# A hybrid decoder layer on one core: recurrent gates' products moved, and the mixer's VectorE and ScalarE work put in a fixed order

## The chip, the cores and the metric

The kernel runs on one core of a Trainium2 chip. The metric is the device time of one execution in microseconds (us), taken as the median of the runs.

## The reference

The layer is a SwiGLU half-step, a token mixer, and a second SwiGLU half-step, each behind an RMS norm, for 512 tokens of width 1024. The change concerns the mixer alone.

```
def hybrid_mixer(h, w_in, ..., w_out):
    z = h @ w_in
    c_val, c_gate, r_x, r_gate = jnp.split(z, [W_CONV, 2 * W_CONV, 2 * W_CONV + W_LRU], axis=-1)
    u = c_val * jax.nn.sigmoid(c_gate)
    u = causal_depthwise_conv(u, conv_dw, conv_dw_bias)            # 31 taps
    u = jax.nn.silu(layernorm(u, conv_ln_g, conv_ln_b))
    xr = causal_depthwise_conv(r_x, lru_conv_w, lru_conv_b)        # 4 taps
    yr = rg_lru(xr, lru_w_a, lru_b_a, lru_w_x, lru_b_x, lru_lambda)
    yr = yr * jax.nn.gelu(r_gate, approximate=True)
    return jnp.concatenate([u, yr], axis=-1) @ w_out

def rg_lru(x, w_a, b_a, w_x, b_x, lam):
    r = jax.nn.sigmoid(block_diag_linear(x, w_a, b_a))
    i = jax.nn.sigmoid(block_diag_linear(x, w_x, b_x))
    log_a = -LRU_C * r * jax.nn.softplus(-lam)
    a = jnp.exp(log_a)
    mult = jnp.sqrt(-jnp.expm1(2.0 * log_a))
    h_t = a_t * h_(t-1) + mult_t * (i_t * x_t)     # a scan over the tokens
```

## The kernel before

Everything is in float32 of which each matrix operand is split into a high half (rounded to the fast matmul type) and a low half (the rest). A product then takes three passes: high by high, high by low, low by high. ScalarE makes the high halves (casts), VectorE the low ones (subtractions). Channels lie on the partitions, in tiles of 128; the mixer has four tiles (c = 0 to 3) of the convolution group and four of the recurrent group, with 512 tokens each. PSUM has eight banks, used in turn by all stages.

The mixer runs in this order on TensorE. First the convolution's gate and value products of the tiles 0, 1 and 2, then the recurrent inputs (`rx_units`), then gate and value of the fourth tile (`zc_units(3)`), all into banks called pz; then the four recurrent gate products (`rg_units`, also pz), called rg0 to rg3 here. In between lie the recurrent gates' small block-diagonal products (pga), which `lru` issues. Last comes the output projection (`out_units`, banks po), first its recurrent half (yhi, ylo by the weight slabs hl), then the convolution's half (uhi, ulo). Between its parts stand the sums over channels with a matrix of ones (pm): the mean, then the variance, of the convolution's output.

The 31 taps of the convolution run on VectorE for the tiles 0, 2 and 3 (`conv_dve`, two PSUM accumulators pc, result cv) and on ScalarE and GpSimd for tile 1 (`conv_pool`). When a VectorE tile has its value product (the product of value bank and gate sigmoid, `val_out`), its taps are queued in `convs`; `step_convs` issues them as long as a planned VectorE clock is behind TensorE's. `lru` is a chain, a generator that is advanced once for each 2.72 us of planned TensorE work: eight gate products (pga) with a sigmoid each (r, i); GpSimd's product xr by i; on ScalarE tanh (th), exponential (r) and square (i); on VectorE the sum th = (i + 1) th; the square root on ScalarE; GpSimd's product xr by th; VectorE's scans (th from r and xr, two tiles a pair); the gating th by gl, where gl is the gelu of the recurrent gate products; the cast yhi and the low half ylo. The constant SCAN_LATER holds the scans back by five such steps. `layernorm` subtracts the mean (cv - pm), squares (sq), takes the variance's root (rs), the reciprocal by token halves, multiplies, applies Silu with gain and bias, casts to uhi and subtracts to ulo.

The calls of `tc.keep_in_program_order` (pin) hold an instruction at the place among the pinned ones of its engine where it is written. All others are placed by a scheduler, by the priority under which they were issued. SP's queue carries the loads of the weight slabs; the slabs of the output projection (wso) and of the second half-step (raw) take their buffers as older slabs come free.

Of the kernel before, what the change touches and what calls it, by code (L numbers as in the profile page):

```python
# [13 lines left out]
P = 128  # L14
# [24 lines left out]
PR_SIDE = -400  # L39
PR_OUT = 300  # L40
PR_COMB = 0
SCAN_LATER = 5
RMS_EPS = 1e-6
LN_EPS = 1e-5
A, B, ALL = (0, HT), (HT, HT), (0, T)
# [30 lines left out]
def layer_kernel(ctx: ExitStack, tc, x, gains, w_g1, w_u1, w_d1a, w_d1b, w_in,  # L76
# [66 lines left out]
    def step_chains():  # L143
        for c in list(chains):
            with tc.high_priority(offset=c[0]):
                if next(c[1], None) is None:
                    chains.remove(c)

    def step_convs():
        while convs and clock["dve"] < clock["pe"]:  # L150
            with tc.high_priority(offset=PR_CONV):
                us = next(convs[0], None)
            if us is None:
                convs.pop(0)
            else:
                dve(us)
# [479 lines left out]
    def zc_units(c, parts):  # L636
        off = ASIDE if len(parts) == 2 else 0
        sgt, sv = Slab(split=ws_in[4 + c], off=off), Slab(split=ws_in[c], off=off)
        box = {}

        def product(key, s, t0, n):
            box[key] = bank("pz")
            mm_feat(box[key][:, :n], s, t0, n, CUT if key == "g" and c == 0 else 0)

        def gate_out(n):
            box["s"] = sp.tile([P, T], F32, name=nm("sgc"), tag="sg", bufs=2)
            S.activation(box["s"][:, :n], box["g"][:, :n], AF.Sigmoid)
# [48 lines left out]
    def conv_dve(c, t0, n):  # L696
        if t0 == 0:
            accs[c] = [bank("pc"), bank("pc")]
        acc, o, at = accs[c], conv_out(c), slice(t0, t0 + n)
        us = 0.66 if n == T else 0.42  # L700
        for j in range(TAPS):
            src, to = mx["ub"][:, c, t0 + j:t0 + j + n], acc[j % 2][:, at]
            if j == 0:
                V.tensor_scalar(out=to, in0=src, scalar1=par(c, P_DW),
                                scalar2=par(c, P_DWB), op0=ALU.mult, op1=ALU.add)
            elif j == 1:
                V.tensor_scalar(out=to, in0=src, scalar1=par(c, P_DW + 1), scalar2=None,
                                op0=ALU.mult)
            else:
                V.scalar_tensor_tensor(out=o[:, at] if j == TAPS - 2 else to, in0=src,  # L710
                                       scalar=par(c, P_DW + j), in1=to,
                                       op0=ALU.mult, op1=ALU.add)
            yield us
        V.tensor_add(o[:, at], acc[0][:, at], o[:, at])
        yield us
        if t0 + n == T:
            conv_done(c)


    def conv_pool(c):  # L720
# [18 lines left out]
    def layernorm():  # L739
# [14 lines left out]
        half = [slice(0, HT), slice(HT, T)]  # L754

        def low(sl):
            for c in range(4):
                v, o = conv_out(c)[:, sl], hi[c // 2][:, c % 2, sl]
                V.tensor_sub(lo[c // 2][:, c % 2, sl], v, o.bitcast(F32))
            dve(1.6)  # L760

        for i, sl in enumerate(half):
            V.reciprocal(rs[:, sl], rs[:, sl])
            dve(1.8)
            for c in range(4):
                v, o = conv_out(c)[:, sl], hi[c // 2][:, c % 2, sl]
                V.tensor_mul(v, v, rs[:, sl])
                S.activation(v, v, AF.Silu, scale=par(c, P_LNG), bias=par(c, P_LNB))
                S.copy(o, v)
            dve(1.6)  # L770
            if i:
                low(half[0])
        low(half[1])
        done["u"] = (hi, lo)

    lr = {}
# [41 lines left out]
            out_.append(Unit([s], 5.44, lambda c=c, s=s: product(c, s), lambda c=c: evac(c)))  # L818
        return out_

    def lru():
        xr, r, i_, th = lr["xr"], two("r"), two("i"), two("th")
        for c in range(4):
            at = (slice(None), c % 2, slice(None))
            for gi, (to, b) in enumerate(((r, P_BA), (i_, P_BX))):
                pga = bank("pga")
                PE.matmul(pga, bd[:, gi, c, :], xr[c // 2][at], start=True, stop=True)
                S.activation(to[c // 2][at], pga, AF.Sigmoid, bias=par(c, b))
            if c % 2:
                yield 1  # L830
        pin = tc.keep_in_program_order
        for q in range(2):
            G.tensor_mul(xr[q], xr[q], i_[q])
            clock["pool"] += 2.4
# [5 lines left out]
            pin(S.activation(r[c // 2][at], r[c // 2][at], AF.Exp, scale=nsp[:, c:c + 1]))  # L840
        for q in range(2):
            pin(S.activation(i_[q], r[q], AF.Square))
        yield 1
        for q in range(2):
            pin(V.scalar_tensor_tensor(out=th[q], in0=i_[q], scalar=1.0, in1=th[q],
                                       op0=ALU.add, op1=ALU.mult))
            dve(1.2)
        for q in range(2):
            S.activation(th[q], th[q], AF.Sqrt)
            G.tensor_mul(xr[q], xr[q], th[q])  # L850
            clock["pool"] += 2.4
        done["roots"] = True
        for _ in range(SCAN_LATER):
            yield 1
        hi, lo = two("yhi", F32R), two("ylo", F32R)
        for q in range(2):
            for c in (2 * q, 2 * q + 1):
                at = (slice(None), c % 2, slice(None))
                pin(V.tensor_tensor_scan(th[c // 2][at], r[c // 2][at], xr[c // 2][at],
# [1 line left out]
                dve(1.2)  # L861
            while ("gl", 2 * q + 1) not in done:
                yield 1
            pin(V.tensor_mul(th[q], th[q], lr["gl"][q]))
            S.copy(hi[q], th[q])
            V.tensor_sub(lo[q], th[q], hi[q].bitcast(F32))
            dve(2.4)
            done["y", q] = (hi, lo)


    def out_units(after):
# [31 lines left out]
        def fin_two():  # L903
            for t in range(2):
# [286 lines left out]
```

## Time and profile before

| | us |
|---|---|
| median of 3 runs | 851.02 (850.5 to 852.06) |
| profiled execution | 851.07 |
| its span, first to last instruction | 849.2 |
| TensorE matmul busy | 833.4 (98%) |
| VectorE busy | 640.5 (75%) |
| ScalarE busy | 425.0 (50%) |
| GpSimd busy | 91.3 (11%) |

The profiled execution is within the range of the runs, and its span is 1.9 us shorter than its time. Busy shares of TensorE count pipelined matmuls, so 98% doesn't tell that it works at its peak. The chain of work that ended last is TensorE for 94% of the span. The mixer lies between about 350 and 508 us.

### The profile page before, as it was taken

What the parts mean: (1) busy time and instruction counts of PE and PEld (TensorE: products, weight loads), DVE (VectorE), ACT (ScalarE), POOL (GpSimd) and SP (SyncE); (2) the same over time, 40 slices, a digit from 0 to 9 for tenths busy, and PEclk for the clock granted to TensorE, in tenths of its full rate; (3) what the DMA queues carried; (4) which work ended last, traced back from release to release, by engine and by line L of the source; (5) the groups of instructions that cost most, each with busy time, mean ns of one, the idle gap of its engine ahead of it and who ended that gap; (6) DMA issues with size and microseconds to landing.
All of it is one profiled execution on the core that took longest, in us unless ns stands there. A gap on an engine that the chain in (4) does not pass through costs nothing.

```text
span 849.2 us, 13877 instructions
## 1 busy us (share of the span) xinstructions
PE 833.4 (98%) x5608; PEld 759.6 (89%) x5608; DVE 640.5 (75%) x931; ACT 425.0 (50%) x677; POOL 91.3 (11%) x114
## 2 busy tenths in 40 slices
PE   8999999999999999999996999999999999999996
PEld 7999989999889998998875789999889998899985
DVE  5989668998658984598977679896548985558844
ACT  7656534666425662335391755555226554136623
POOL 2001110000110001209740010000000000000001
PEclk9999999999999999999998999999999999999998
DMA  7447895555985579655541032334312334223302
GB/s 266 172 149 261 310 324 198 195 176 174 313 329 182 193 242 375 226 203 194 198 140 59 0 100 70 101 104 150 123 45 86 120 123 152 74 76 100 124 26 100
DMA packets 36722, 139.14 MB, mean 164 GB/s; under 512 B 5041, under 2 KB 5169, under 8 KB 33970
## 3 DMA queue, kind: packets, MB, share of 16 engines
q1 hardware_dynamic: 29170, 112.04, 38.9%
q0 software_dynamic: 6912, 25.17, 7.7%
q8 instruction: 44, 0.72, 0.3%
q10 hardware_dynamic: 576, 1.05, 0.3%
q14 instruction: 20, 0.16, 0.1%
HBM read 110.98 MB, written 27.26 MB: 163 GB/s over the span
## 4 chain that ended last, share of the span: by engine, by line
PE 94%; DVE 2%; ACT 1%; DMA 1%; SPq 0%; issue 0%; POOLq 0%; POOL 0%; ACTq 0%
PE px L331 25%; PE pz L331 12%; PE pz L316 8%; PE pd L557 8%; PE pd L558 8%; PE pd L559 8%; PE pw L331 6%; PE pgate L316 3%; PE pup L316 3%; PE po L557 2%; PE po L559 2%; PE po L558 2%; PE pdl L559 1%; PE pdl L557 1%; PE pdl L558 1%; DMA xt<-in_x 1%
## 5 line engine op out<-in xcount | busy, mean ns | idle before, releaser
L215 DVE TENSOR_TENSOR hl<-raw,hl 128x1024 fp32r<-128x1024 f32 (+1 forms) x132 | 139.8, 1061 | 40.3 <-ACT hl L206 26.8
L215 DVE TENSOR_TENSOR hl<-tt,hl 128x1024 fp32r<-128x1024 f32 x78 | 94.9, 1216 | 34.8 <-ACT hl L242 21.1
L331 PE MATMUL px<-sx,hl 128*128 128x256 f32 x936 | 118.8, 276 | 0.0
L331 PE MATMUL pz<-sx,hl 128*128 128x256 f32 x936 | 118.8, 276 | 0.0
L557 PE MATMUL pd<-hl,act 128*128 128x512 f32 x304 | 118.6, 390 | 0.0
L558 PE MATMUL pd<-hl,act 128*128 128x512 f32 x304 | 118.4, 389 | 0.0
L559 PE MATMUL pd<-hl,act 128*128 128x512 f32 x304 | 118.3, 389 | 0.0
L331 PEld LDWEIGHTS pz<-sx,hl 128*128 128x128 f32 x936 | 111.9, 188 | 0.0
L331 PEld LDWEIGHTS px<-sx,hl 128*128 128x128 f32 x936 | 111.9, 188 | 0.0
L331 PE MATMUL px<-h_hi,hl 128*128 128x256 f32 x630 | 96.9, 277 | 0.0
L242 ACT CAST hl<-tt 128x1024 fp32r<-128x1024 f32 x78 | 81.8, 1051 | 26.4 <-PE pd L559 20.3
L331 PEld LDWEIGHTS px<-h_hi,hl 128*128 128x128 f32 x630 | 83.7, 188 | 1.4 <-DVE um L529 0.7
L242 ACT CAST hl<-raw 128x1024 fp32r<-128x1024 f32 x78 | 65.1, 835 | 38.9 <-PE pd L559 26.3
L206 ACT CAST hl<-raw 128x1024 fp32r<-128x1024 f32 x54 | 56.1, 1051 | 46.5 <-PE pd L559 39.7
L559 PEld LDWEIGHTS pd<-hl,act 128*128 128x128 f32 x304 | 57.1, 188 | 11.9
L557 PEld LDWEIGHTS pd<-hl,act 128*128 128x128 f32 x304 | 57.1, 188 | 11.5
L558 PEld LDWEIGHTS pd<-hl,act 128*128 128x128 f32 x304 | 57.1, 188 | 11.4
L316 PE MATMUL pz<-h_hi,hl 128*128 128x512 f32 (+2 forms) x322 | 63.0, 346 | 0.0
L710 DVE SCALAR_TENSOR_TENSOR pc<-sx,ch,pc 128x256 f32<-128x256 f32 (+1 forms) x112 | 61.4, 615 | 0.1
L316 PEld LDWEIGHTS pz<-h_hi,hl 128*128 128x128 f32 x322 | 51.7, 188 | 7.9 <-issue 0.5
L300 DVE TENSOR_TENSOR slo<-sraw,shi 128x1024 fp32r<-128x1024 f32 x24 | 29.3, 1219 | 28.0 <-ACT shi L299 28.0
L331 PE MATMUL px<-h_lo,hl 128*128 128x256 f32 x312 | 48.2, 277 | 0.0
(186 smaller groups left out, 1317.1 us busy)
## 6 DMA issues: line engine op xcount, KB each, us to landing
raw<-in_w_g SPq DMA_DIRECT2D x44, 512.0 KB, 3.5
raw<-in_w_u SPq DMA_DIRECT2D x44, 512.0 KB, 4.4
hl<-wsi SPq DMA_DIRECT2D x16, 1024.0 KB, 4.8
sraw<-in_w_in SPq DMA_DIRECT2D x16, 512.0 KB, 6.4
wsi<-shi POOLq DMA_DIRECT2D x16, 512.0 KB, 5.2
wsi<-slo POOLq DMA_DIRECT2D x16, 512.0 KB, 5.5
raw<-in_w_d1a SPq DMA_DIRECT2D x16, 512.0 KB, 4.7
raw<-in_w_d2a SPq DMA_DIRECT2D x16, 512.0 KB, 3.5
```

What stands on the lines that cost most here:

```text
L206: return S.copy(s.hi, s.raw)
L215: ins = V.tensor_sub(s.lo, s.raw, s.hi.bitcast(F32))
L242: S.copy(s.hi, s.raw)
L300: V.tensor_sub(lo, raws[-1], hi.bitcast(F32))
L316: ins = PE.matmul(ps[:, c0:c1], w[:, k, :], h[:, k, t0 + c0:t0 + c1], start=(i == 0 and k == 0), stop=(i == 2 and k == KT - 1))
L331: PE.matmul(ps[:, c0:c1], w[:, k * P:(k + 1) * P], h[:, k, c0:c1], start=(first and i == 0 and k == 0), stop=(i == 2 and k == 3), skip_gro ...
L557: PE.matmul(ps, ahi, whi, start=first, stop=False)
L558: PE.matmul(ps, ahi, wlo, start=False, stop=False)
L559: PE.matmul(ps, alo, whi, start=False, stop=last)
L710: V.scalar_tensor_tensor(out=o[:, at] if j == TAPS - 2 else to, in0=src, scalar=par(c, P_DW + j), in1=to, op0=ALU.mult, op1=ALU.add)
```

## The change

Four things change, all in the mixer. (1) When the fourth tile has its value product, all taps still queued are issued, and the chain `lru` is put up and advanced at once, so that the eight gate products stand directly behind the fourth tile's on TensorE, and before rg0. (2) The fourth tile's taps are handed to `lru` as a generator and pinned; `lru` issues them in fixed numbers between its own steps: 17 before the sums, four before the first pair of scans, one before the first gating, two before each low half, the rest at the end. SCAN_LATER is gone. (3) The second pair's output products of tokens 0 and 1 are one unit, and the mean stands behind it, so the variance is 12 matmuls later too. (4) In `layernorm` the steps are pinned; each tile's Silu and cast follow each other, the first low half comes before the second half's reciprocal and the rest of the first half's low parts before the second half's products; a small activation on 16 columns loads the Silu table directly behind the variance's root. The sigmoid of the convolution's gate also gets a higher priority.

```diff
     def val_out(t0, n):
             V.tensor_mul(mx["ub"][:, c, 30 + t0:30 + t0 + n], box["v"][:, :n], box["s"][:, :n])
             dve(0.7)
-            if c != 1:
+            if c == 3:
+                while convs:
+                    step_conv()
+                chains.append((PR_LRU, lru(conv_dve(c, t0, n))))
+                step_chains()
+            elif c != 1:
                 convs.append(conv_dve(c, t0, n))
             elif t0 + n == T:
                 pool_convs.append(conv_pool(c))
-            if c == 3:
-                chains.append((PR_LRU, lru()))
...
         rs = sp.tile([P, T], F32, name=nm("rs"), tag="sg", bufs=2)
-        S.activation(rs, var, AF.Sqrt, bias=lneps)
+        tc.keep_in_program_order(S.activation(rs, var, AF.Sqrt, bias=lneps))
+
+        junk = sp.tile([P, 16], F32, name=nm("ss"), tag="ss", bufs=4)
+        tc.keep_in_program_order(S.activation(junk, ones[:, 0:16], AF.Silu))
...
-        for i, sl in enumerate(half):
-            V.reciprocal(rs[:, sl], rs[:, sl])
-            dve(1.8)
-            for c in range(4):
...
-            if i:
-                low(half[0])
-        low(half[1])
+        h0, h1 = slice(0, HT), slice(HT, T)
+        pin(V.reciprocal(rs[:, h0], rs[:, h0]))
+        high(h0)
+        low(h0, (0,))
+        pin(V.reciprocal(rs[:, h1], rs[:, h1]))
+        low(h0, (1, 2, 3))
+        high(h1)
+        low(h1, range(4))
...
-    def lru():
+
+    def lru(conv):
+        def taps(n):
+            for us in (next(conv, None) for _ in range(n)):
+                dve(us or 0.0)
...
             pin(S.activation(i_[q], r[q], AF.Square))
-        yield 1
+        taps(17)
         for q in range(2):
             pin(V.scalar_tensor_tensor(out=th[q], in0=i_[q], scalar=1.0, in1=th[q],
...
-        for _ in range(SCAN_LATER):
-            yield 1
         hi, lo = two("yhi", F32R), two("ylo", F32R)
         for q in range(2):
+            taps(0 if q else 4)
             for c in (2 * q, 2 * q + 1):
...
             while ("gl", 2 * q + 1) not in done:
                 yield 1
+            taps(0 if q else 1)
             pin(V.tensor_mul(th[q], th[q], lr["gl"][q]))
-            S.copy(hi[q], th[q])
-            V.tensor_sub(lo[q], th[q], hi[q].bitcast(F32))
+            pin(S.copy(hi[q], th[q]))
+            taps(2)
+            pin(V.tensor_sub(lo[q], th[q], hi[q].bitcast(F32)))
             dve(2.4)
             done["y", q] = (hi, lo)
+        taps(TAPS)
+        yield 1
...
         out_ = [Unit(sy, 5.44, lambda: part((0, 1), sy, ("y", 0), True, (0, 1))),
-                Unit(sy, 2.72, lambda: part((0,), sy, ("y", 1), True, (2, 3))),
-                Unit([], 0.0, mean),
-                Unit(sy, 2.72, lambda: part((1,), sy, ("y", 1), True, (2, 3)))]
+                Unit(sy, 5.44, lambda: part((0, 1), sy, ("y", 1), True, (2, 3))),
+                Unit([], 0.0, mean)]
```

How it moves the instructions, at three places. On TensorE around the gates' products before (pz_4512 is the fourth tile's value product, pz_4550 is rg0, pz_4645 is rg1):

```order
L316 MATMUL pz_4512<-h_hi,hl_4329 128x512 x8
L316 MATMUL pz_4550<-h_hi,hl_4376 128x512 x8
L316 MATMUL pz_4550<-h_lo,hl_4376 128x512 x8
L316 MATMUL pz_4550<-h_hi,hl_4376 128x512 x8
L827 MATMUL pga_4581<-xr_4275,bd 128x512
L827 MATMUL pga_4584<-xr_4275,bd 128x512
L827 MATMUL pga_4587<-xr_4275,bd 128x512
L827 MATMUL pga_4590<-xr_4275,bd 128x512
L827 MATMUL pga_4605<-xr_4276,bd 128x512
L827 MATMUL pga_4608<-xr_4276,bd 128x512
L827 MATMUL pga_4611<-xr_4276,bd 128x512
L827 MATMUL pga_4614<-xr_4276,bd 128x512
```

And there after the change (pz_4636 is rg0):

```order
L318 MATMUL pz_4512<-h_hi,hl_4329 128x512 x8
L849 MATMUL pga_4560<-xr_4275,bd 128x512
L849 MATMUL pga_4563<-xr_4275,bd 128x512
L849 MATMUL pga_4566<-xr_4275,bd 128x512
L849 MATMUL pga_4569<-xr_4275,bd 128x512
L849 MATMUL pga_4572<-xr_4276,bd 128x512
L849 MATMUL pga_4575<-xr_4276,bd 128x512
L849 MATMUL pga_4578<-xr_4276,bd 128x512
L849 MATMUL pga_4581<-xr_4276,bd 128x512
L318 MATMUL pz_4636<-h_hi,hl_4376 128x512 x8
L318 MATMUL pz_4636<-h_lo,hl_4376 128x512 x8
L318 MATMUL pz_4636<-h_hi,hl_4376 128x512 x8
```

The eight gate products and the 24 matmuls of rg0 have changed places; nothing else moves on TensorE up to the output projection.

On VectorE from the last tap before the first pair of scans to the second low half, before (pc are the fourth tile's taps, the row of cv_4317 from pc_4601 is its last sum):

```order
L710 SCALAR_TENSOR_TENSOR pc_4602<-sx_478_3865,ch,pc_4602 128x512
L859 SCALAR_TENSOR_TENSOR th_4579<-r_4575,xr_4275 128x512 x2
L710 SCALAR_TENSOR_TENSOR pc_4602<-sx_478_3865,ch,pc_4602 128x512
L864 TENSOR_TENSOR th_4579<-th_4579,gl_4548 128x1024
L710 SCALAR_TENSOR_TENSOR pc_4602<-sx_478_3865,ch,pc_4602 128x512
L710 SCALAR_TENSOR_TENSOR cv_4317<-sx_478_3865,ch,pc_4602 128x512
L866 TENSOR_TENSOR ylo_4744<-th_4579,yhi_4742 128x1024
L859 SCALAR_TENSOR_TENSOR th_4580<-r_4576,xr_4276 128x512 x2
L714 TENSOR_TENSOR cv_4317<-pc_4601,cv_4317 128x512
L864 TENSOR_TENSOR th_4580<-th_4580,gl_4549 128x1024
L866 TENSOR_TENSOR ylo_4745<-th_4580,yhi_4743 128x1024
```

And after, from the last tap before the scans:

```order
L716 SCALAR_TENSOR_TENSOR pc_4596<-sx_478_3865,ch,pc_4596 128x512
L877 SCALAR_TENSOR_TENSOR th_4558<-r_4554,xr_4275 128x512 x2
L716 SCALAR_TENSOR_TENSOR pc_4597<-sx_478_3865,ch,pc_4597 128x512
L883 TENSOR_TENSOR th_4558<-th_4558,gl_4634 128x1024
L716 SCALAR_TENSOR_TENSOR pc_4596<-sx_478_3865,ch,pc_4596 128x512
L716 SCALAR_TENSOR_TENSOR pc_4597<-sx_478_3865,ch,pc_4597 128x512
L886 TENSOR_TENSOR ylo_4624<-th_4558,yhi_4622 128x1024
L877 SCALAR_TENSOR_TENSOR th_4559<-r_4555,xr_4276 128x512 x2
L883 TENSOR_TENSOR th_4559<-th_4559,gl_4635 128x1024
L716 SCALAR_TENSOR_TENSOR pc_4596<-sx_478_3865,ch,pc_4596 128x512
L716 SCALAR_TENSOR_TENSOR pc_4597<-sx_478_3865,ch,pc_4597 128x512
L886 TENSOR_TENSOR ylo_4625<-th_4559,yhi_4623 128x1024
```

Between the sums (th from i) and the first scans there stood eleven taps, now four; 17 taps stand before the sums as they did, and six operations of the fourth tile, its last sum included, now follow the second low half.

On ScalarE from the variance's root to the casts of the second half-step's first weights, before (cv to uhi; hl from raw):

```order
L750 ACTIVATE rs_4874<-pm_4869,lneps 128x512
L768 ACT_TABLE_LOAD
L768 ACTIVATE cv_3990<-cv_3990,ch 128x256 x2
L769 CAST uhi_4888<-cv_3990 128x256 x2
L768 ACTIVATE cv_4317<-cv_4317,ch 128x256 x2
L769 CAST uhi_4889<-cv_4317 128x256 x2
L768 ACTIVATE cv_3990<-cv_3990,ch 128x256 x2
L769 CAST uhi_4888<-cv_3990 128x256 x2
L768 ACTIVATE cv_4317<-cv_4317,ch 128x256 x2
L769 CAST uhi_4889<-cv_4317 128x256 x2
L206 CAST hl_4972<-raw_4754 128x1024
```

And after, up to the last of these casts:

```order
L763 ACT_TABLE_LOAD
L763 ACTIVATE ss_4888<-ones 128x16
L772 ACTIVATE cv_3990<-cv_3990,ch 128x256
L773 CAST uhi_4916<-cv_3990 128x256
L772 ACTIVATE cv_3990<-cv_3990,ch 128x256
L773 CAST uhi_4916<-cv_3990 128x256
L772 ACTIVATE cv_4317<-cv_4317,ch 128x256
L208 CAST hl_4974<-raw_4754 128x1024
L773 CAST uhi_4917<-cv_4317 128x256
L772 ACTIVATE cv_4317<-cv_4317,ch 128x256
L208 CAST hl_4976<-raw_4756 128x1024
L773 CAST uhi_4917<-cv_4317 128x256
```

Two more hl casts follow, and then the second half's eight rows. The hl casts, which stood behind both halves, now stand within and behind the first.

## Rows read from the trace of the kernel before

**Rows 1.** TensorE's waits, whole execution: us in total, times, longest.

```profile
PE po L557 <- ACT yhi L865: 6.4, 1, 6.4
PE pgate L316 <- ACT hl L206: 1.1, 1, 1.1
PE idle L954 <- DVE warm L946: 1.0, 1, 1.0
PE ptr L369 <- DVE xn L359: 0.2, 1, 0.2
```

**Rows 2.** TensorE's timeline: start, us, instruction, count [idle before <-releaser].

```profile
416.85 3.79 PE L316 MATMUL pz<-h_hi,hl 128*128 128x512 f32 x16
...
424.11 7.03 PE L827 MATMUL pga<-xr,bd 128*128 128x512 f32 x16
...
445.51 1.97 PE L316 MATMUL pz<-h_hi,hl 128*128 128x512 f32 x8
453.93 0.80 PE L557 MATMUL po<-hl,yhi 128*128 128x512 f32 x1 [6.45 <-ACT yhi L865]
...
458.91 0.39 PE L559 MATMUL po<-hl,ylo 128*128 128x512 f32 x1
...
464.62 1.02 PE L677 MATMUL pm<-cs,ones 128*128 128x512 f32 x2
...
469.34 3.59 PE L677 MATMUL pm<-sq,ones 128*128 128x512 f32 x8
...
483.44 0.39 PE L557 MATMUL po<-hl,uhi 128*128 128x512 f32 x1
```

**Rows 3.** Stretches after the pause: length, busy time by engine, PEclk, DMA share, GB/s.

```profile
453.90:458.90 5.00, 4.97 (x11) 3.61 (x12) 5.00 (x6) 0.47 (x1) 0.00 (x0) 0.51 0.00 0
458.90:464.00 5.10, 5.10 (x24) 4.18 (x23) 1.67 (x2) 1.05 (x1) 0.00 (x0) 1.00 0.00 0
```

**Rows 4.** VectorE's timeline, columns as in group 2.

```profile
418.93 0.69 DVE L650 TENSOR_TENSOR sx<-pz,sgc 128x512 f32<-128x512 f32 x1 [1.00 <-PE pz L316]
...
422.29 0.69 DVE L714 TENSOR_TENSOR cv<-pc,cv 128x512 f32<-128x512 f32 x1
...
439.17 2.36 DVE L845 SCALAR_TENSOR_TENSOR th<-i,th 128x1024 f32<-128x1024 f32 x2 [3.58 <-ACT i L842]
441.45 7.33 DVE L710 SCALAR_TENSOR_TENSOR pc<-sx,ch,pc 128x512 f32<-128x512 f32 x11
448.70 2.33 DVE L859 TENSOR_TENSOR_SCAN th<-r,xr 128x512 f32<-128x512 f32 x2
...
451.58 1.22 DVE L864 TENSOR_TENSOR th<-th,gl 128x1024 f32<-128x1024 f32 x1
...
480.12 0.76 DVE L759 TENSOR_TENSOR ulo<-cv,uhi 128x256 fp32r<-128x256 f32 x2 [0.44 <-ACT uhi L769]
...
496.02 1.28 DVE L353 SCALAR_TENSOR_TENSOR xn<-xt,ss,gbc 128x1024 f32<-128x1024 f32 x1 [0.82 <-POOL ss L347]
```

**Rows 5.** ScalarE's timeline, columns as in group 2.

```profile
425.23 0.69 ACT L828 ACTIVATE r<-pga,ch 128x512 f32<-128x512 f32 x1 [11.21 <-PE pga L827]
...
440.11 1.28 ACT L849 ACT_TABLE_LOAD   x1
441.40 2.01 ACT L849 ACTIVATE th<-th 128x1024 f32<-128x1024 f32 x2
...
452.83 1.04 ACT L865 CAST yhi<-th 128x1024 fp32r<-128x1024 f32 x1 [6.53 <-DVE th L864]
```

**Rows 6.** GpSimd's timeline, columns as in group 2.

```profile
442.61 4.77 POOL L850 TENSOR_TENSOR xr<-xr,th 128x1024 f32<-128x1024 f32 x2 [8.26 <-ACT th L849]
495.12 0.22 POOL L344 TENSOR_SCALAR ss<-ss 128x1 f32<-128x1 f32 x1 [47.74 <-ACT xn L341]
...
496.48 0.91 POOL L344 TENSOR_SCALAR ss<-ss 128x1 f32<-128x1 f32 x1 [0.49 <-ACT xn L341]
```

More of the change, by code (lines that the diff above doesn't have):

```diff
@@ L41 @@
 PR_COMB = 0
-SCAN_LATER = 5
 RMS_EPS = 1e-6
@@ L147, in step_chains, with step_conv @@
                     chains.remove(c)
+    def step_conv():
+        with tc.high_priority(offset=PR_CONV):
+            us = next(convs[0], None)
+        if us is None:
+            convs.pop(0)
+        else:
+            dve(us)
     def step_convs():
         while convs and clock["dve"] < clock["pe"]:
[L151 to L156, printed above, removed]
+            step_conv()
         while pool_convs and clock["pool"] < clock["pe"]:
@@ L646, in gate_out @@
             box["s"] = sp.tile([P, T], F32, name=nm("sgc"), tag="sg", bufs=2)
-            S.activation(box["s"][:, :n], box["g"][:, :n], AF.Sigmoid)
+            with tc.high_priority(offset=PR_OUT):
+                S.activation(box["s"][:, :n], box["g"][:, :n], AF.Sigmoid)
         def val_out(t0, n):
@@ L703, in conv_dve @@
             if j == 0:
-                V.tensor_scalar(out=to, in0=src, scalar1=par(c, P_DW),
-                                scalar2=par(c, P_DWB), op0=ALU.mult, op1=ALU.add)
+                ins = V.tensor_scalar(out=to, in0=src, scalar1=par(c, P_DW),
+                                      scalar2=par(c, P_DWB), op0=ALU.mult, op1=ALU.add)
             elif j == 1:
-                V.tensor_scalar(out=to, in0=src, scalar1=par(c, P_DW + 1), scalar2=None,
-                                op0=ALU.mult)
-            else:
-                V.scalar_tensor_tensor(out=o[:, at] if j == TAPS - 2 else to, in0=src,
-                                       scalar=par(c, P_DW + j), in1=to,
-                                       op0=ALU.mult, op1=ALU.add)
+                ins = V.tensor_scalar(out=to, in0=src, scalar1=par(c, P_DW + 1),
+                                      scalar2=None, op0=ALU.mult)
+            else:
+                ins = V.scalar_tensor_tensor(out=o[:, at] if j == TAPS - 2 else to, in0=src,
+                                             scalar=par(c, P_DW + j), in1=to,
+                                             op0=ALU.mult, op1=ALU.add)
+            if c == 3:
+                tc.keep_in_program_order(ins)
             yield us
-        V.tensor_add(o[:, at], acc[0][:, at], o[:, at])
-        yield us
+        ins = V.tensor_add(o[:, at], acc[0][:, at], o[:, at])
+        if c == 3:
+            tc.keep_in_program_order(ins)
         if t0 + n == T:
             conv_done(c)
+        yield us
     def conv_pool(c):
@@ L753, in layernorm, with high, low @@
         hi, lo = two("uhi", F32R), two("ulo", F32R)
-        half = [slice(0, HT), slice(HT, T)]
-        def low(sl):
+        pin = tc.keep_in_program_order
+        def high(sl):
             for c in range(4):
                 v, o = conv_out(c)[:, sl], hi[c // 2][:, c % 2, sl]
-                V.tensor_sub(lo[c // 2][:, c % 2, sl], v, o.bitcast(F32))
+                pin(V.tensor_mul(v, v, rs[:, sl]))
+                pin(S.activation(v, v, AF.Silu, scale=par(c, P_LNG), bias=par(c, P_LNB)))
+                pin(S.copy(o, v))
             dve(1.6)
-        for i, sl in enumerate(half):
-            V.reciprocal(rs[:, sl], rs[:, sl])
-            dve(1.8)
-            for c in range(4):
+        def low(sl, cs):
+            for c in cs:
                 v, o = conv_out(c)[:, sl], hi[c // 2][:, c % 2, sl]
[L767 to L770, printed above, removed]
-            if i:
-                low(half[0])
-        low(half[1])
+                pin(V.tensor_sub(lo[c // 2][:, c % 2, sl], v, o.bitcast(F32)))
+                dve(0.4)
+        h0, h1 = slice(0, HT), slice(HT, T)
[6 more added lines that the diff above has]
+        low(h1, range(4))
         done["u"] = (hi, lo)
@@ L827, in lru @@
                 PE.matmul(pga, bd[:, gi, c, :], xr[c // 2][at], start=True, stop=True)
-                S.activation(to[c // 2][at], pga, AF.Sigmoid, bias=par(c, b))
-            if c % 2:
-                yield 1
-        pin = tc.keep_in_program_order
+                pin(S.activation(to[c // 2][at], pga, AF.Sigmoid, bias=par(c, b)))
         for q in range(2):
@@ L848, in lru @@
         for q in range(2):
-            S.activation(th[q], th[q], AF.Sqrt)
+            pin(S.activation(th[q], th[q], AF.Sqrt))
             G.tensor_mul(xr[q], xr[q], th[q])
```

3 lines of the change are left out of this document (2 added, 1 removed).

## The prediction

> **What bounds the kernel now.** I read the waits of TensorE first: in the whole execution it waits for data once for long, 6.4 us at the first output product (po) for the rounded high half yhi; the other three waits, 1.1 us and less, belong to the first microseconds of the program, where the first weights are cast (pgate), a constant is set (idle) and the first tokens are transposed (ptr) [rows 1]. All else on the path is matmul work, so a gain has to come from this place and what hangs on it. The timeline of TensorE puts the place between 445.51 and 453.93 us [rows 2]. The last eight matmuls of the fourth gate product begin at 445.51; a full-rate 128x512 matmul follows the one before it by (3.79 - 0.39) / 15 = 0.227 us (sixteen in 3.79 us, 0.39 us the last one's own length), so the next could begin at 445.51 + 8 x 0.227 = 447.33. It begins at 453.93: 6.60 us lost. Then the clock: in the 5 us after the pause TensorE was granted 0.51, its lower level, and in the next stretch 1.00 again [rows 3]. The first 11 po matmuls take 453.93 to 458.91, 4.98 us where 11 x 0.227 = 2.49 would do: another 2.49 us. The pause costs 9.09 us together.
>
> Why yhi is late, backwards: the cast ran at 452.83 after 6.53 us of idle ScalarE, waiting for VectorE's gating at 451.58 [rows 4, 5]. VectorE had scans at 448.70 and eleven taps before them from 441.45, without a gap, though GpSimd's two products, the scans' input, were done at 442.61 + 4.77 = 447.38 [rows 4, 6]. Before that VectorE had waited 3.58 us, to 439.17, for ScalarE's squares, whose chain begins at the gates' sigmoids at 425.23, after 11.21 us of idle ScalarE waiting for the gates' products (pga) at 424.11 [rows 2, 4, 5]. So VectorE is idle early and overfull late.
>
> **The change part by part.** The same arithmetic remains on TensorE; ScalarE gets one tiny activation that loads the Silu table. No DMA is added, and SP's and GpSimd's instructions keep their order.
>
> *Gates' products earlier.* They move from behind the first recurrent gate product (rg0) to before it. rg0 begins at 416.85 + 8 x 0.227 = 418.66, so pga starts 424.11 - 418.66 = 5.45 us earlier, and everything of ScalarE's chain with it: sigmoids from 419.8, squares done (where the table load starts) at 440.11 - 5.45 = 434.66, square roots from 441.40 - 5.45 = 435.95 if VectorE is ready [rows 2, 5]. For TensorE the swap is free; rg0 to rg3 still end at 447.33. What is new: the last three of the eight pga banks come free with VectorE's value product (done 418.93 + 0.69 = 419.62), the third tile's last tap, and its final sum (422.29 + 0.69 = 422.98) [rows 4]. All eight products take 7.03 us [rows 2], 0.88 each at most, so TensorE asks for the last bank at about 418.66 + 7 x 0.86 = 424.7 and for the one before at 423.8 (free at about 422.3): 1.5 us of slack, cost nothing. Two wso transfers wait for rg0's slab, 6.5 us later than now; the first is used only after 447.3.
>
> *Fixed order on VectorE.* The fourth tile's taps (0.66 us each: eleven in 7.33) start at about 422.9 [rows 4]. As before, 17 of them stand before the two sums (th), but nothing else holds VectorE up: 422.9 + 17 x 0.66 = 434.1; the squares are there by 434.66, and the first one a us earlier, so no wait: sums 434.1 to 436.5 (2.36 us). Roots 435.95 to 437.96, GpSimd's products 442.61 - 5.45 = 437.16 to 441.93, the first done at about 439.55 [rows 4 to 6]. Four taps, not eleven, stand before the scans and fill VectorE to 439.1; the first pair of scans can start at 439.6.
>
> Then two cases. *Free:* the scans run beside GpSimd's second product: scans 2.33 us to 441.9, one tap, gating 1.22 to 443.7, cast 1.04 to 444.8, low half (two taps ahead of it) 445.0 to 446.2. TensorE wants yhi at 447.33 and ylo, at its fourth matmul, at 448.0. No wait. *Held:* the scans start when GpSimd's second product is over, at 441.95. All is 2.35 us later: yhi at 447.15, still in time; ylo at 448.55, so TensorE waits 0.55 us. The second pair follows in a row: scans to 450.85, gating 452.0, cast 453.1 (TensorE wants it at 447.33 + 0.55 + 24 x 0.227 = 453.32), two taps, low half at 454.5, wanted at 453.8: 0.7 us. The hold costs 1.25 us in all.
>
> No row of before has a scan, or any VectorE operation on two SBUF tensors, beside a long GpSimd operation. From below: the taps, which read one SBUF and one PSUM tensor, ran at 0.66 us beside the same products, cost 0 [rows 4, 6]. From above: a GpSimd 128x1 add that takes 0.22 us took 0.91 where VectorE's L353, two SBUF inputs, ran from 496.02 to 497.30; it ended at 497.39 [rows 4, 6]. The scans read two SBUF tensors (r and xr), like L353, so I take the hold, 1.25 us. A gain below the free case is excluded: TensorE has no idle left there.
> The Trainium skill, "SBUF — State Buffer", section "SBUF: two separate sides", calls the port pair that VectorE and GpSimd share an exclusive lock, kept for a whole instruction by whichever starts first, VectorE's two-SBUF-input operations included. The L353 row agrees for VectorE first; by the rule GpSimd's second product, which follows the first without a gap, shuts the scans out, and the sum is 843.2, without it 842.0.
>
> *Mean and variance later.* The mean now stands behind all 48 matmuls of tokens 0 and 1. The fourth tile's last sum comes six VectorE operations after the second low half: 454.5 + 6 x 0.66 = 458.5; TensorE reaches the mean at 453.32 + 0.7 + 5.44 = 459.5, 1.0 us of cover (free case: 456.1 against 458.2). If that cover is gone, each us late is a us of TensorE. Between mean and variance stand 13 matmuls as now (464.62 to 469.34), so that distance stays without a pause [rows 2].
>
> *Low halves by halves.* From the variance to the first product with uhi TensorE takes 483.44 - 469.34 = 14.10 us now; 12 matmuls fewer lie between in the new order, so 14.10 - 2.72 = 11.38. In the old order the first low half begins 480.12 - 469.34 = 10.78 us after the variance product and lasts 0.4: even that would meet the demand (the third matmul, 11.8) [rows 2, 4]. In the new order it does not wait for the second reciprocal and the four products of the second half, and the table load is taken out of the way, so I count several us of cover and cost 0. Queued behind the new waits: ScalarE's casts of the next weights (hl) now stand between the halves and wait for TensorE's last read of the old slabs, in the last quarter of the output products before u. The third tile's high half is behind the first of them. TensorE wants it 5.4 us after u begins, and the cast (about 1 us) is released before u begins: covered.
>
> *What is late next.* Nothing that the trace shows: from 506 us on TensorE has no data wait at all: all that it has in the execution are the four of [rows 1], one here and three at the start, so what is gained is kept to the end.
>
> **Sum.** The profiled execution took 851.07 us (span 849.2), the median of the runs is 851.02. 851.07 - 6.60 - 2.49 + 1.25 = 843.2 held; 842.0 free.
>
> **The rivals.** *Free scans*, 842.0 us: the taps beside GpSimd speak for it, the L353 row against. Chance 0.3.
> *A rest of the wait.* The chain from pga to yhi has some ten hand-overs that I took from the old spacing; in the held case yhi is only 0.2 us early. One that comes 1 to 4 us later than counted leaves so long a pause, 844 to 847 us. Against it: the same rows show such hand-overs at 0.03 to 0.06 us. Chance 0.12.
> *Slower, at the gates' banks.* If VectorE came late with the value product and the third tile's sum, TensorE would stand before the gates, with the four gate products queued behind. Past 1.5 us of slack every us is lost whole; it takes 1.5 + 7.9 = 9.4 us of lateness to lose the gain, and 12 us of it would give 843.2 + 10.5 = 853.7, before the lower clock that such a pause brings with it. Against it: VectorE was idle 1.00 us before the value product, waiting for TensorE [rows 4], and its order up to that sum is not changed. Chance 0.03.
> *It does not bite*: yhi is held by something that the old trace hides and comes when it did, 851 us. Against it: gating ends at 452.80, the cast begins at 452.83 and ends at 453.87, and TensorE goes on at 453.93 [rows 2, 4, 5]. Chance 0.03.
>
> **How the numbers follow.** Forecast 0.52, free 0.30, rest 0.12, no bite 0.03, slower 0.03. The range runs from just below the free case to the middle of the rest: 841.0 to 846.0, holding about 0.9 by these chances; I don't cut it closer, since the hand-overs are estimates. A measurement tells about 0.2% (1.7 us) from no change: faster 0.94, same 0.03, slower 0.03.
>
> **What would show it.** Right: no TensorE wait over 1 us at po, a granted clock of 1.00 between 447 and 475, u beginning near 475, pga near 418.7, the th sums without idle. Scans starting at 439.6 mean free, at 442 held. Wrong: a wait of TensorE at pm for the fourth tile, at po for ylo longer than 1 us, or at pga; or new waits after u.

## The result and the profile after

The changed kernel takes 844.01 us (median of four runs: 845.38, 845.05, 842.98, 842.69) beside 850.82 us for the kernel before in the same session; the ratio is 0.9918, 95% interval 0.9895 to 0.994. The forecast was 843.2 us, the range 841.0 to 846.0. In a second session four more runs of the same program gave a median of 843.12 us (843.0 to 843.47), ratio 0.9895, 0.9881 to 0.991.

TensorE's waits after (engine, line, for what: us in total, times, longest). The wait for yhi of [rows 1] is gone, two short ones for low halves are new:

```profile
PE idle L975 <- DVE warm L967: 1.0, 1, 1.0
PE po L561 <- DVE ylo L886: 0.8, 2, 0.5
```

TensorE's timeline after, the answer to [rows 2] (start, us, instruction, count, idle before it):

```profile
420.85 7.03 PE L849 MATMUL pga<-xr,bd 128*128 128x512 f32 x16
...
447.69 1.98 PE L318 MATMUL pz<-h_hi,hl 128*128 128x512 f32 x8
449.50 0.39 PE L559 MATMUL po<-hl,yhi 128*128 128x512 f32 x1
...
450.58 0.50 PE L561 MATMUL po<-hl,ylo 128*128 128x512 f32 x1 [0.23 <-DVE ylo L886]
...
456.61 0.50 PE L561 MATMUL po<-hl,ylo 128*128 128x512 f32 x1 [0.53 <-DVE ylo L886]
...
461.73 1.02 PE L683 MATMUL pm<-cs,ones 128*128 128x512 f32 x2
...
466.45 3.59 PE L683 MATMUL pm<-sq,ones 128*128 128x512 f32 x8
...
477.82 0.39 PE L559 MATMUL po<-hl,uhi 128*128 128x512 f32 x1
```

The first output product now follows the last gate product without a gap: 449.50 - 447.69 = 1.81 us for eight matmuls. The clock stays at its higher level (2.4 GHz) where [rows 3] had 0.51 (windows: length, busy time by engine, PEclk, DMA share, GB/s):

```profile
447.40:453.00 5.60, 5.37 (x24) 4.10 (x24) 5.50 (x7) 2.14 (x3) 0.00 (x0) 1.00 0.55 211
453.00:458.90 5.90, 5.37 (x24) 4.13 (x23) 5.90 (x8) 1.06 (x1) 0.00 (x0) 1.00 0.11 44
```

VectorE, GpSimd and ScalarE after, the answers to [rows 4 to 6]. The sums follow the taps without idle; the first pair of scans takes 4.51 us where it took 2.33:

```profile
436.33 2.35 DVE L864 SCALAR_TENSOR_TENSOR th<-i,th 128x1024 f32<-128x1024 f32 x2
438.60 2.73 DVE L716 SCALAR_TENSOR_TENSOR pc<-sx,ch,pc 128x512 f32<-128x512 f32 x4
441.79 4.51 DVE L877 TENSOR_TENSOR_SCAN th<-r,xr 128x512 f32<-128x512 f32 x2 [0.46 <-POOL xr L869]
...
449.31 1.22 DVE L886 TENSOR_TENSOR ylo<-th,yhi 128x1024 fp32r<-128x1024 f32 x1
450.44 2.33 DVE L877 TENSOR_TENSOR_SCAN th<-r,xr 128x512 f32<-128x512 f32 x2
...
455.34 1.22 DVE L886 TENSOR_TENSOR ylo<-th,yhi 128x1024 fp32r<-128x1024 f32 x1
```

```profile
439.35 4.75 POOL L869 TENSOR_TENSOR xr<-xr,th 128x1024 f32<-128x1024 f32 x2 [6.70 <-ACT th L868]
```

```profile
438.14 2.01 ACT L868 ACTIVATE th<-th 128x1024 f32<-128x1024 f32 x2
...
448.11 1.05 ACT L884 CAST yhi<-th 128x1024 fp32r<-128x1024 f32 x1 [5.55 <-DVE th L883]
```

**Where the 0.8 us over the forecast are.** The whole mixer lies 2.2 us later in this execution than the prediction's times: pga at 420.85, not 418.66. That comes from the first microseconds, whose code is the same in both kernels. TensorE's timeline of the first microseconds (g and idle are products that the program issues at its start), kernel before:

```profile
4.33 2.20 PE L959 MATMUL g<-grow,warm 1*128 1x512 f32 x4
6.46 0.94 PE L954 MATMUL idle<-warm 128*128 128x128 f32 x6
```

the profiled execution of the changed kernel:

```profile
4.32 3.78 PE L980 MATMUL g<-grow,warm 1*128 1x512 f32 x4
8.03 1.65 PE L975 MATMUL idle<-warm 128*128 128x128 f32 x6
...
11.18 1.49 PE L975 MATMUL idle<-warm 128*128 128x128 f32 x6
...
13.89 0.83 PE L975 MATMUL idle<-warm 128*128 128x128 f32 x6
```

and the changed kernel in the second session, where pga then begins at 418.87:

```profile
4.33 2.26 PE L980 MATMUL g<-grow,warm 1*128 1x512 f32 x4
6.52 0.94 PE L975 MATMUL idle<-warm 128*128 128x128 f32 x6
```

The same matmuls take nearly twice as long in some executions; the profiled one with the slow matmuls took 845.4 us, the other 843.5. In the slow one six idle products take 1.65 and 1.49 us up to 13 us and 0.83 us at 13.89, so TensorE reaches its full pace later; the granted clock that the profile shows is 1.00 in both kinds of execution, and no run shows what decides. The runs of the kernel before fall into two groups as well (17 runs of a later session: 850.51 to 851.19 and 852.21 to 853.6 us). To leave the start out I compare programs by one distance in the trace, from the last eight matmuls of the gate products (445.51 in [rows 2], 447.69 above) to the first output product with uhi. Before: 483.44 - 445.51 = 37.93 us. After: 477.82 - 447.69 = 30.13 us. The gain is 7.80 us; the prediction said 9.09 - 1.25 = 7.84. Between the medians it is 6.81 us in the first session and 9.40 us in the second (852.52 to 843.12), since the two kinds of start fall differently on the two kernels. But for the start, what lies outside this distance hardly differs: in the second session's execution of the changed kernel the last eight begin at 445.71, and from the first product with uhi to the end of the span all profiled executions of this study take 365.7 to 366.0 us.

### The profile page after: what moved, and what is told of

Same layout as the page of the kernel before. It is cut to its first block, busy times and chain, and to the rows that moved or that the text cites. A ratio compares the mean times of both kernels' runs of the same rounds, so it can differ in the third digit from the quotient of the medians.

```text
span 843.6 us, 13881 instructions
## 1 busy us (share of the span) xinstructions
PE 834.8 (99%) x5608; PEld 761.4 (90%) x5608; DVE 642.6 (76%) x931; ACT 425.9 (50%) x678; POOL 92.1 (11%) x114
## 4 chain that ended last, share of the span: by engine, by line
PE 96%; DVE 2%; ACT 1%; issue 0%; POOL 0%; POOLq 0%; DVEq 0%; ACTq 0%
PE px L333 25%; PE pz L333 13%; PE pd L559 8%; PE pd L561 8%; PE pd L560 8%; PE pz L318 8%; PE pw L333 6%; PE pgate L318 3%; PE pup L318 3%; PE po L561 2%; PE po L559 1%; PE po L560 1%; PE ptr L371 1%; PE pdl L560 1%; PE pdl L559 1%; PE pdl L561 1%
## 5 line engine op out<-in xcount | busy, mean ns | idle before, releaser
L301 ACT CAST shi<-sraw 128x1024 fp32r<-128x1024 f32 x24 | 25.3, 1052 | 46.0 <-DMA sraw<-in_w_in 24.2
```

The lines of the kernel that those rows point to most:

```text
L301: S.copy(hi, raws[-1])
```

## The experiments

All are made from the changed kernel, except gates_only. The last column is that distance.

| kernel | what differs | median, us | runs, us | distance, us |
|---|---|---|---|---|
| before | | 850.82 to 853.06 | | 37.93 |
| after, after_again | | 844.01, 843.12 | 842.69 to 845.38 | 30.13, 30.17 |
| gates_only | before, gates moved | 845.86 | 845.66 to 847.5 | 32.51 |
| gates_late | gates not moved | 851.38 | 848.2 to 852.68 | 36.92 |
| gates_and_order | old mean and norm | 843.08 | 842.91 to 845.1 | 30.15 |
| mean_early | old place of the mean | 845.08 | 844.68 to 845.54 | 30.11 |
| norm_old | old norm | 844.93 | 843.0 to 845.25 | 30.13 |
| pool_extra | one GpSimd product more | 847.18 | 844.83 to 847.4 | 31.80 |
| eight_taps | eight taps before the scans | 844.04 | 842.45 to 844.55 | 29.16 |
| eight_warm | and a longer start | 843.32 | 842.17 to 844.76 | 29.14 |
| twelve_taps | twelve taps | 847.47 | 845.48 to 848.93 | 33.54 |
| fourteen_taps | fourteen taps | 848.97 | 847.91 to 850.07 | 34.79 |

**The changed kernel again.** 

> The changed kernel once more, to see whether its start differs between executions. Theory 'start': the 2.2 us by which the profiled run was late before the fourth tile come from the first 15 us, where the same matmuls took 3.78 us (g) and 1.65 us (six idle ones) against 2.20 and 0.94; then the runs fall again into groups near 842.8 and 845.2, and the profiled execution of whichever group shows the gates' products (pga) near 418.7 or near 420.85, with the same distances behind it: scans 20.9 us, rounded high half 27.3 us and first output product 28.65 us after the first gates' product. Rival 'layout': the changed program itself starts slower; then pga is near 420.9 in every profile and no run comes under 844.5.

Measured: g 2.26 us, pga 418.87, distance 30.17; all four runs at 843.0 to 843.5. The same program starts in either way, so the late start is no part of the change: "layout" falls.

**The gates alone.** Added to the kernel before:

```
                 chains.append((PR_LRU, lru()))
+                step_chains()
...
                 S.activation(to[c // 2][at], pga, AF.Sigmoid, bias=par(c, b))
-            if c % 2:
-                yield 1
```

> The kernel before with one thing changed: all eight gates' products are issued at once behind the fourth tile's value product, ahead of the first recurrent gate product. Order of the taps, mean and norm are left as the scheduler had them. Theory 'the gates carry it': the sums come 15.1 us behind the first gates' product, then four taps, the scans held until GpSimd's second product ends at 22.8, rounded high half at 26.6 to 27.6, wanted at 28.65: the 6.6 us pause and the lower clock are gone, TensorE waits at most 1 us for low halves and at most 1 us for the fourth tile's sum at pm; 843 to 845 us. Theory 'the fixed order is needed too': VectorE places taps so that scans or low halves come 3 us or more later, TensorE waits 2 us or more at po, and the time is 846 us or more.

Measured: distance 32.51, 5.42 us of the 7.80. The first pair of scans comes as in the changed kernel, after four taps; but the scheduler puts three taps between the second pair and its gating, so the second yhi is late (timelines of VectorE, then TensorE):

```profile
450.37 2.04 DVE L711 SCALAR_TENSOR_TENSOR pc<-sx,ch,pc 128x512 f32<-128x512 f32 x3
```

```profile
454.72 0.50 PE L557 MATMUL po<-hl,yhi 128*128 128x512 f32 x1 [1.19 <-ACT yhi L864]
456.05 0.50 PE L559 MATMUL po<-hl,ylo 128*128 128x512 f32 x1 [0.59 <-DVE ylo L865]
```

The mean on TensorE and the fourth tile's last sum on VectorE, here and then in gates_and_order:

```profile
458.47 1.02 PE L678 MATMUL pm<-cs,ones 128*128 128x512 f32 x2
460.77 0.69 DVE L715 TENSOR_TENSOR cv<-pc,cv 128x512 f32<-128x512 f32 x1
```

```profile
456.67 1.02 PE L683 MATMUL pm<-cs,ones 128*128 128x512 f32 x2
457.52 0.69 DVE L722 TENSOR_TENSOR cv<-pc,cv 128x512 f32<-128x512 f32 x1
```

Neither theory is quite right: the gates carry most, and the fixed order is worth 32.51 - 30.15 = 2.36 us on top. SCAN_LATER's end and the sigmoid's priority come with it; no run parts them from it. Of the 2.36 us, 1.71 lie between the first output product and the mean (447.23 to 458.47 here, 447.14 to 456.67 in gates_and_order), where the second half of y is, which the expectation had not counted, and 0.65 behind it, where the fourth tile's last sum comes at 460.77 and not at 457.52.

**The order alone.** The changed kernel without the line that issues the gates at once:

```
                 chains.append((PR_LRU, lru(conv_dve(c, t0, n))))
-                step_chains()
```

> The changed kernel with only the gates' products put back behind the first recurrent gate product; fixed order of taps, scans and gating, later mean and norm by halves are kept. Theory: with the gates 5.45 us later the first output product is possible 23.2 us behind them; sums at 15.1, scans done at 24.9, rounded high half at 27.9: a pause of 4.7 us at po, again followed by some 5 us at the lower clock (another 2.5 us), and 0.8 us for the low halves: 850 us, 1 us better than before. If such a pause leaves the clock alone, 847.5 us. Rival 'the order carries it': the pause is under 2 us and the time under 846 us.

Measured: 4.98 us of pause, the lower level (1.2 GHz) behind it, distance 36.92, 1.01 us better than before. The sum is as expected, its parts are not quite: the expectation had 4.7 us of pause, 2.5 for the clock and 0.8 for the low halves; the trace has 4.98, 3.0 (worked out below) and no wait for the low halves. The profiled execution took 852.01 us with the late start (g 3.78 us). TensorE's timeline, and the window behind the pause (columns as above):

```profile
454.50 0.79 PE L559 MATMUL po<-hl,yhi 128*128 128x512 f32 x1 [4.98 <-ACT yhi L883]
...
468.37 1.02 PE L682 MATMUL pm<-cs,ones 128*128 128x512 f32 x2
```

```profile
454.50:459.50 5.00, 5.00 (x12) 3.69 (x13) 4.90 (x6) 0.94 (x3) 0.00 (x0) 0.50 0.00 0
```

Alone the order gains 1.01 us, the gates 5.42; together 7.80, 1.37 more than the sum. What the rows show of it: of the 2.36 us that the order gains over gates_only, 1.71 lie at the second half of y, where gates_only waits 1.19 and 0.59 us; before and in gates_late TensorE waits in the mixer only at the first output product, so there is no such wait for the order to save. Twelve runs spread from 848.2 to 852.68 us, more than the start explains. The mean granted clock was 0.995 to 0.997 in the three runs of 848.2 to 848.6 us and 0.992 to 0.994 in the other nine, so the lower level may have lasted less long in those three; only one of the nine was profiled, so that stays open.

**Mean and norm.** Old places put back one at a time, then both (the old code of those lines in the diff ahead):

```
-                Unit(sy, 5.44, lambda: part((0, 1), sy, ("y", 1), True, (2, 3))),
-                Unit([], 0.0, mean)]
+                Unit(sy, 2.72, lambda: part((0,), sy, ("y", 1), True, (2, 3))),
+                Unit([], 0.0, mean),
+                Unit(sy, 2.72, lambda: part((1,), sy, ("y", 1), True, (2, 3)))]
```

> The changed kernel with the mean back between the third and the fourth quarter of tokens 0 and 1, as before. Theory 'cover': the fourth tile's last sum ends 39.7 us behind the first gates' product, TensorE reaches the mean 2.72 us earlier than in the changed kernel, at 38.2: it waits 1.5 us there (pm for the fourth tile), and the time rises by 1.5 us, more if the clock falls after it. Rival 'nothing': the move is worth nothing in the new order, the sum is there in time, 0.0 us.

> The changed kernel with the old norm: no early load of the Silu table, low halves in one piece behind both halves' products, as before. Theory 'covered': the first low half begins 10.8 us after the variance's first matmul, as in the kernel before, wanted at 11.8: no wait, 0.0 us. Rival 'the norm became the next limit': with 12 matmuls fewer between variance and output products of u, a hand-over is late and TensorE waits 0.5 to 2 us at the first product with ulo; the time rises by that.

> The changed kernel with mean and norm both as before; only the gates' products and the fixed order remain of the change. Theory: each of the two was worth 0.0 alone, so both together are worth 0.0: the first product with uhi begins 57.0 us behind the first gates' product, as in the changed kernel. Rival 'one covers for the other': with both old TensorE waits 0.5 us or more between 458 and 485 us.

Measured: 30.11, 30.13 and 30.15. None of them is worth anything here; the medians of the first two, 845.08 and 844.93 us, are those of the late start, which their profiled executions have (g 3.78 us in both). "Cover" fell for the mean: TensorE does come early, but it does not stand. In mean_early the scheduler puts output products between the two halves of the mean (TensorE's timeline):

```profile
458.66 1.02 PE L683 MATMUL pm<-cs,ones 128*128 128x512 f32 x2
459.12 0.80 PE L559 MATMUL po<-hl,yhi 128*128 128x512 f32 x1
...
460.45 1.02 PE L683 MATMUL pm<-cv,ones 128*128 128x512 f32 x2
```

The fourth tile's last sum ran from 459.55 to 460.24 there; its mean product, at 460.45, is 0.2 us behind it. VectorE's timeline there:

```profile
459.55 0.69 DVE L722 TENSOR_TENSOR cv<-pc,cv 128x512 f32<-128x512 f32 x1
```

**The scans and GpSimd.** Two tests of the hold, one that takes the meeting away and one that makes it longer. First more taps ahead of the scans:

```
-            taps(0 if q else 4)
+            taps(0 if q else 8)
...
-            taps(0 if q else 1)
...
-            taps(2)
+            taps(2 if q else 1)
```

> Eight taps instead of four before the first pair of scans, none between scans and gating, one instead of two before the first low half. Theory 'held': the scans took 4.51 us only because GpSimd's second product ran; here they start after it, 23.6 us behind the first gates' product, take 2.33 us, the low half comes at about 27.9 us where it is wanted at 29.3, and the second one is about 0.7 us earlier than now, which is 0.2 us early: both waits at po (0.23 and 0.53 us) are gone, 0.76 us less than the changed kernel. Theory 'the scans are slow by themselves' (after taps, or at that place): 4.51 us again, gating ends at 29.3, the cast at 30.4, TensorE waits about 1.7 us at po and the time is 1 us or more above the changed kernel's.

Measured: pga is at 420.85 as in the changed kernel's profile, so the times compare directly. The scans start at 443.86, when GpSimd is about to end, and take 2.47 us; the profile lists no wait of TensorE at po. VectorE's timeline and TensorE's waits in the whole execution:

```profile
443.86 2.47 DVE L877 TENSOR_TENSOR_SCAN th<-r,xr 128x512 f32<-128x512 f32 x2
```

```profile
PE idle L974 <- DVE warm L966: 1.0, 1, 1.0
PE pgate L318 <- DVE hl L217: 0.2, 1, 0.2
```

The distance is 29.16, 0.97 us less than the changed kernel's. The scans are not slow by themselves. A little of the cost of the low halves is left: TensorE's timeline has the second low half 0.22 us late (0.45 us from the matmul before it, where 0.227 is the full pace):

```profile
455.64 0.39 PE L560 MATMUL po<-hl,yhi 128*128 128x512 f32 x1
456.09 0.50 PE L561 MATMUL po<-hl,ylo 128*128 128x512 f32 x1
```

With eight_warm, which has the same order, it is the best version of the study by the trace. The medians (844.04, and 843.12 for the changed kernel in that session) do not show it, since the two kinds of start differ by twice as much: its profiled execution, 844.55 us, has the late start, that of the changed kernel the early one.

Then one more product on GpSimd, with no operand in common with the scans:

```
-            G.tensor_mul(xr[q], xr[q], th[q])
+            pin(G.tensor_mul(xr[q], xr[q], th[q]))
             clock["pool"] += 2.4
+        pin(G.tensor_mul(i_[1], i_[1], i_[1]))
```

> The changed kernel with one more GpSimd product of the same size (128x1024, on a tile nobody needs any more, also in SBUF) right behind GpSimd's second product. Theory 'held': the scans cannot start before GpSimd stops; the pair takes 4.51 + 2.38 = 6.9 us, the rounded high half ends 30.85 us behind the first gates' product instead of 28.2 to 28.6, TensorE waits 2.2 us there and 0.8 us at each low half: 3 us above the changed kernel, up to 5.5 if the clock falls after the pause. Theory 'something else': the scans have no operand in common with that product, 4.51 us again and no difference.

Measured: the pair takes 6.17 us, so "something else" falls, but it is not the 6.9 us expected. VectorE's and GpSimd's timelines:

```profile
441.88 6.17 DVE L878 TENSOR_TENSOR_SCAN th<-r,xr 128x512 f32<-128x512 f32 x2 [0.47 <-POOL xr L869]
```

```profile
439.43 4.77 POOL L869 TENSOR_TENSOR xr<-xr,th 128x1024 f32<-128x1024 f32 x2 [6.70 <-ACT th L868]
444.14 2.83 POOL L871 TENSOR_TENSOR i<-i 128x1024 f32<-128x1024 f32 x1
```

The four scans apart (their line: least, median and longest in ns, first and last start), here and in the changed kernel:

```profile
L878 DVE TENSOR_TENSOR_SCAN th<-r,xr x4: 1192/2028/3402, 441.9 to 453.3; 128x512 f32<-128x512 f32 x4
```

```profile
L877 DVE TENSOR_TENSOR_SCAN th<-r,xr x4: 1194/1206/3397, 441.8 to 451.6; 128x512 f32<-128x512 f32 x4
```

The first scan takes 3.40 us in both: 2.2 us held and 1.19 of its own, ending at 445.28, 1.1 us behind GpSimd's second product (444.20). The extra product does not keep it out; the second scan then ends at 448.05, 1.08 us behind the extra product (446.97). So a scan waits out the GpSimd product that runs when it comes; it looks as if the two take turns. The Trainium skill, "SBUF — State Buffer", section "SBUF: two separate sides", states an exclusive lock: a VectorE operation with two SBUF inputs and a GpSimd operation that reads SBUF want the same port pair, and whichever starts first keeps it for its whole instruction. These runs agree for the scans. They agree less for GpSimd: its extra product lasts 2.83 us, 0.45 more than its sister's 2.38, while a scan ran in its first 1.14 us; GpSimd's spans in a profile are rough, so whether it was shut out for longer stays open. The distance rose by 1.67 us, not by 3: the pair grew by 1.66, and yhi had 0.3 us to spare (cast done at 449.16, wanted at 449.50), while the low halves cost 0.3 us more than in the changed kernel (12.53 us, not 12.23, from the first output product to the mean).

**Shorter pauses and the clock.** Twelve and fourteen taps ahead of the first scans make shorter pauses on purpose:

```
-            taps(0 if q else 4)
+            taps(0 if q else 12)
```

> The changed kernel with twelve taps instead of four before the first pair of scans, to make a middle pause on purpose. By the order: scans from 25.7 to 28.0 us behind the first gates' product (not held, GpSimd ended at 23.3), gating to 29.9, cast to 31.0, first output product possible at 28.65: a pause of about 2.3 us, low halves 0.7 and 0.5. Theory 'the lower clock comes with any pause above some 1.2 us' (1.21 us left it at 1.00, 4.98 us and 6.45 us were followed by 0.50): the matmuls behind the pause start every 0.43 us for some microseconds, and the product with uhi comes 57.0 + 2.75 + 2.5 = 62.2 us behind the gates. Theory 'only the long pauses do it': 0.227 us spacing, 59.7.

> The same with fourteen taps before the first scans: pause about 3.7 us, low halves about 0.8 and 0.5. With the lower clock behind it the product with uhi comes 57.0 + 4.2 + 2.5 = 63.7 us behind the gates' first product, without it 61.2. If twelve taps leave the clock alone and these don't, the change lies between the two pauses.

Measured: the pauses are 2.08 and 3.33 us; uhi comes 60.4 and 61.6 us behind the gates' first product, between the two expectations, since the lower level did follow both, but for a shorter time. In both a second wait of 0.5 us, at ylo, lies between the first output product and the matmuls at the lower level, so the runs do not show what the first wait alone would do. TensorE with twelve taps, its first output product and the windows behind it:

```profile
449.35 0.50 PE L559 MATMUL po<-hl,yhi 128*128 128x512 f32 x1 [2.08 <-ACT yhi L884]
```

```profile
449.30:451.10 1.80, 1.26 (x4) 0.79 (x5) 1.80 (x3) 0.98 (x3) 0.00 (x0) 1.00 1.01 428
451.10:454.60 3.50, 3.50 (x10) 2.74 (x9) 3.12 (x3) 0.18 (x1) 0.00 (x0) 0.53 0.08 33
454.60:458.00 3.40, 3.40 (x16) 2.76 (x16) 1.23 (x1) 0.86 (x1) 0.00 (x0) 0.98 0.00 0
```

The price of the lower level is the time from the first output product to the mean, less that of the same 48 matmuls at the full pace (48 x 0.227 = 10.90 us) and less the gap at ylo: 462.75 - 449.35 - 10.90 - 0.65 = 1.9 us with twelve taps, 464.14 - 450.75 - 10.90 - 0.68 = 1.8 us with fourteen, 468.37 - 454.50 - 10.90 = 3.0 us in gates_late, and with 36 matmuls 464.62 - 453.93 - 8.17 = 2.5 us before. Of each figure some 0.1 us for each wait is not the clock's: the matmul behind a wait takes 0.34 us and not 0.227 also where the granted clock stays at 1.00 (450.58 to 450.92 in the changed kernel). The pauses of 1.21 us (pool_extra, 0.41 us more at ylo) and 1.19 us (gates_only, 0.59 us more) left the granted clock at 1.00.

**The start.** eight_taps with IDLE = (9, 3, 3, 3) instead of (7, 3, 3, 3):

> The kernel with eight taps, and nine instead of seven idle products (18 instead of 14 passes) at the very start. Executions so far came in two groups about 2 us apart: where the four g matmuls took 1.98 to 2.26 us the time was lower, where they took 3.78 us higher. Theory 'a longer start settles it': g takes about 2.2 us in every execution and all runs come within 842.5 to 843.3. Rival 'it is not ours to set': two groups again, 842.4 to 843.0 and 844.3 to 845.3, each up to 0.9 us later for the longer start.

Measured: 842.17, 842.24, 844.4 and 844.76 us, the profiled one (844.4) again with g in 3.78 us. Two groups, so a longer start by this much does not settle it; what does stays open.

## Why the prediction was right, point by point

- **The pause and the clock, 9.09 us.** Right: no wait for yhi, clock 1.00, and undoing the gates brings 4.98 us of the pause and 3.0 us of the clock back. In size too: the gain and what the low halves take of it are 7.80 + 1.33 = 9.13 us.
- **Gates earlier, chain shifted with them.** Right. Counted from the first gates' product: sums at 15.44 us predicted, 436.33 - 420.85 = 15.48 measured; GpSimd's products from 18.50 to 23.27, measured 18.50 to 23.25; yhi ready at 28.49, measured 449.16 - 420.85 = 28.31. The banks cost nothing: no TensorE wait at pga.
- **The hold, 1.25 us.** Right in kind, shown by eight_taps and pool_extra. The low halves cost 461.73 - 449.50 - 10.90 = 1.33 us in the changed kernel. The two gaps at ylo are 450.58 - 449.96 - 0.227 = 0.39 and 456.61 - 455.70 - 0.227 = 0.68 us, where 0.55 and 0.7 were counted; the slower matmul behind each, 0.11 us more than the full pace, was not counted. That the two errors nearly cancel is luck. Eight taps win 0.97 of the 1.33 us back. The rival "free scans" was wrong, and the row that had decided was a far one, a 128x1 add beside L353 in [rows 4, 6].
- **Fixed order.** It was treated as one thing with the gates. The runs part them: 5.42 us for the gates alone, 2.36 for the order on top, through the second gating and not the first.
- **Mean later.** The cover of 1.0 us was about right (the sum ends at 39.7, TensorE comes at 461.73 - 420.85 = 40.88). The sentence that each us late would be a us of TensorE was not put to the test: with the mean 2.72 us earlier nothing was lost, since four output products stand before the product that needs the sum, which is then 0.2 us early.
- **Low halves by halves.** Cost 0, right; the old norm costs 0 as well, so this part of the change was not needed for the gain.
- **The sum.** 7.84 us predicted, 7.80 measured over the mixer. What the sum left out is the start: made against an execution with the early start, it forecast 843.2, which the runs with that start show (842.69 to 843.47); the first session's four runs are half of the other kind. How many runs of a session start late is chance, and so is how near a median comes to the forecast within these 2 us.

## What to carry to other kernels

When one engine waits long for a chain that goes through three others, look at where in the chain an engine is idle early and full late; moving the few instructions that start the chain was worth 5.42 of 7.80 us here, and a fixed order on the full engine, which came to little without the first (1.01 us), the rest. Count VectorE's scans, which read two SBUF tensors, as waiting for the long GpSimd product that runs beside them, and put other work there (eight taps instead of four: 0.97 us). Compare variants by a distance in the trace when a start or an end that is not theirs moves by more than the effect.

## What the runs showed that I had not expected

- The start differs between executions of one program by about 2 us: the four g matmuls take 1.98 to 2.26 or 3.78 us, while the granted clock in the profile's windows is 1.00 in both.
- A scan held by GpSimd waits for the running product only (3.40 us, 1.19 of its own); the next product, which starts right behind, does not keep it out.
- The lower clock level cost 1.8 to 1.9 us behind pauses of 2.08 and 3.33 us, each with a second wait of 0.5 us, 2.5 us behind 6.45 us and 3.0 us behind 4.98 us; it did not come behind 1.19 and 1.21 us.
- An early request on TensorE's side need not be a wait: four output products slipped in between the mean's two halves.
